# Value and gate panels as 512-column products, and another kind of unread product in the norms

## The chip, the cores and the metric

The kernel runs on one core of a Trainium2 chip. A core has TensorE (PE in the profile; its weight loads are listed as PEld), VectorE (DVE), ScalarE (ACT), GpSimd (POOL), and SyncE (SP), which here only issues DMAs. The metric is the device time of one execution in microseconds (us). The kernel before takes 2851.77 us, the median of 3 runs (2851.21 to 2854.91).

## The reference

256 tokens of width 1024 pass through two networks, one after the other. The first has two layers: multi-scale retention with a SwiGLU feed-forward, then a dilated attention with a second feed-forward, with a layer norm after each part. The second has two layers of a mixer (attention of 8 heads with forget gates, a 31-tap convolution, a gated linear recurrence) and a layer of 16384 small experts ("peer") of which each token uses 128, with rms norms ahead of them and one at the end. Cut to what the change touches:

```
retention:  q, k, v, gate = split(x @ w_in)        # gate and v: 4 heads x 512 columns
            y = norm(retain(rope(q), rope(k), v));  out = (silu(gate) * y) @ w_out
attention:  q, k, v of 3 groups x 16 heads x 64;    softmax over all keys of the 3 groups
mixer:      q, k, v = x @ w_in[:, :1536]            # 8 heads x 64 columns each
            out = concat(attend(q, k, v, f), conv, rnn) @ w_out
layer_norm: (x - mean) * rsqrt(var + eps) * g + b;  rms_norm: x * rsqrt(mean(x^2) + eps) * g
```

## The kernel before, in words

**Products.** Each float32 operand is split into two float32r parts, hi and lo (ScalarE rounds hi, VectorE subtracts to get lo), and a product is three float32r products: hi x hi, lo x hi, hi x lo. Weights come as panels [128, 1024] of 512 KB in the order of their use (class `Stream`): SyncE loads up to 4 ahead into `raw`, then `whi` and `wlo` have three buffers each. `W.ahead` emits the split of a later panel between the products of the present one.

Four shapes of product share the panels. `feat` gives features by tokens: the panel is stationary, 256 tokens move, 24 products per panel into one half of a bank. `nat` gives tokens by features for values and gates: the tokens are stationary, 256 columns of the panel move, two panels of 4 k-blocks make [2 halves of the tokens x 256 columns] in one bank, 24 products per panel, `mm(o, l[:, k, t], r[:, s], ...)`. `krow` and `krow_tail` are the sums over rows: 512 columns move, 12 products per panel, into four banks `acc`. There are 40 `nat` panels of x in retention (32) and the two mixers (4 each), and 24 in the attention.

**Banks.** `bank()` hands out two banks named `w` in turn for `feat`, `nat` and the unread products; a bank can be written again once its last reader (an ACTIVATE of 512 elements on ScalarE) is done. `sbank`, `spare` and `aux` are the other banks, for the small products.

**Order.** The program is emitted in the order of the main products. Small chains of work (a head's softmax, the convolution, the recurrence) are generators; `chains.run()`, called inside `feat` (3 times a panel), `nat` (4 times) and `krow` (2 times), emits a step of a chain when an estimate of time (`Clock`) says that its inputs are done. So where a step stands on each engine is decided by that estimate, and nothing is reordered later.

**Mixer.** `MIX_ORDER = "FCRAB"`: forget gate, convolution, recurrence, then A (queries and keys of heads pairs 0 and 1, then a `nat` for half of the values) and B (queries and keys of pairs 2 and 3, then a `nat` for the other half). The chains `heads(hp, ...)` of pairs 0 and 1 are added before A's `nat`, those of 2 and 3 before B's. Then come the `krow` products of the mixed features in the order `MIX_REST = (0, 1, 6, 7, 4, 5, 2, 3)` (0 to 3 heads, 4 and 5 convolution, 6 and 7 recurrence), the last three in `krow_tail`.

**Norms.** After each sum the tokens are normed on VectorE, ScalarE and GpSimd, transposed by TensorE, and copied from the banks by ScalarE into `xh` (four copies of [128, 4 blocks, 128 tokens]). While TensorE has nothing to do, `keep_warm(n)` gives it products that nobody reads, `mm(ps[:, :128], ident, ident, ...)` in float32: 14 in each layer norm (`WARM_LN`, the one that feeds mixer 0 among them), 8 in each other rms norm (`WARM_RMS`). In a layer norm they stand ahead of all transposes, in an rms norm between the transposes of the first 128 tokens and those of the others. The profile counts each of these as two instructions.

Of the kernel before, what the change touches and what calls it, by code (L numbers as in the profile page):

```python
# [13 lines left out]
AF = mybir.ActivationFunctionType  # L14
# [14 lines left out]
WARM_START = 18  # L29
LEAD = 2.4  # L30
# [3 lines left out]
EARLY = (0, 1)  # L34
# [15 lines left out]
class Stream:  # L50
    """Weight panels [128, 1024] in the order of their use: loaded ahead, split ahead into
    two float32r parts whose sum is the float32 panel."""
# [36 lines left out]
    def open(self, n):  # L89
        """The first panel, in n pieces."""  # L90
        self.step = 1024 // n
        for parts, name, dt, bufs in ((self.raw, "raw", F32, self.R), (self.hi, "whi", F32R, self.B),
                                      (self.lo, "wlo", F32R, self.B)):
            parts[0] = self.pool.tile([128, 1024], dt, name=name, bufs=bufs)
        self.nd = self.nh = self.nl = 1
# [13 lines left out]
    def ahead(self, part):  # L109
        """Further panels' parts, while the one that was got last is in use."""  # L110
# [5 lines left out]
    def take(self, k):  # L116
        """k panels to be used in any order, k at most the number of buffers."""
        self.lo_to(self.n + k)
        return [self._next() for _ in range(k)]
# [7 lines left out]
class Clock:  # L127
    """An estimate of when the instructions emitted so far are done, from their sizes, the order on
    their engines and the data they share."""
# [7 lines left out]
    def place(x):  # L137
        """The elements of a partition, as runs: their starts and their length."""
# [15 lines left out]
    def freed(self, slot, last):  # L154
        """When a bank's last tile has been read."""
# [57 lines left out]
class Timed:  # L213
    """An engine whose instructions the clock takes note of."""
# [23 lines left out]
class Chains:  # L238
    """Chains of work woven between the main products: a chain goes on when the clock says that its
    last step is done."""  # L240
# [4 lines left out]
    def add(self, gen, lane=None, rank=1, need=0):  # L245
        """Chains of a lane run one after the other; lower ranks go first. need: banks for the next step."""
# [42 lines left out]
def net(tc, A, out, stop=None):  # L289
# [3 lines left out]
    with ctx:  # L293
# [21 lines left out]
        def choice():  # L315
            """The chains' banks, by when they are free; while the sums' banks are unused, two of them also serve."""
# [54 lines left out]
        def feat(ps, xh, xl):  # L371
            """ps[feature, token] of one panel: weights stationary, tokens moving."""
# [8 lines left out]
        def nat(ps, xh, xl):  # L381
            """ps[token, c, 256 columns], K = 1024, two panels of 4 k-blocks."""
# [14 lines left out]
    
        def krow(acc, ah, al, first=False):
            """acc[c][half] += a^T panel for one k-block a [128, tokens] against 1024 columns."""
# [10 lines left out]
        def krow_tail(acc, parts, first=False):  # L410
            """The last three panels of such a sum, the first tokens before the others."""
# [17 lines left out]
        def rsqrt_wide(dst, v, a, b):  # L429
            """dst = 1 / sqrt(v): a first guess from the exponent, one step of second and one of third order."""  # L430
# [14 lines left out]
        class Turned:  # L445
            """xh, xl from the tokens' rows: the first part at once, the second in the end."""
# [18 lines left out]
        def to_T_flipped(c, h, dh, dl, src):  # L465
            """As to_T, the tokens from last to first."""
# [8 lines left out]
        def keep_warm(n):  # L475
            """Products nobody reads: the tensor engine's clock falls when it has nothing to do."""
            ps = bank()
            for _ in range(n):
                mm(ps[:, :128], ident, ident, start=True, stop=True)
# [3 lines left out]
        class Layer:  # L483
            """Layer norm of ALPHA times xN plus acc, in place."""
# [27 lines left out]
            def scale_beside(self, c, h):  # L512
                """As scale, on the other engines."""
# [40 lines left out]
        class Root:  # L554
            """xn[c] = rms norm of xN."""
# [24 lines left out]
        def rms(gb, xn, acc=None, then=None, first=None):  # L580
            """xn[c] = rms norm of xN, to which acc is added first; or of a layer norm."""
# [47 lines left out]
        # ------------------------------------------------------------------ retention  # L629
        def retention():  # L630
            with tc.tile_pool(name="ret", bufs=1) as p:
# [27 lines left out]
                def project(h):  # L659
# [7 lines left out]
                    for nm, f in (("v", AF.Copy), ("g", AF.Silu)):  # L667
                        r[nm] = p.tile([128, 2, 512], F32, name=nm + "_", bufs=2)
                        for j in range(2):
                            ps = bank()  # L670
                            nat(ps, xh, xl)
                            nc.scalar.activation(r[nm][:, :, j * 256:(j + 1) * 256],
                                                 ps.rearrange("p (c n) -> p c n", c=2), f)
# [66 lines left out]
        # ------------------------------------------------------------------ feed-forward  # L740
# [43 lines left out]
        # ------------------------------------------------------------------ dilated attention  # L784
        def bias_tiles(p):
            """scr[16 group + head, n]: the bias at distance n - 127, with the group's mask."""
# [18 lines left out]
        def attention(scr, xrh, xrl):  # L805
            """The three groups of a head share one softmax: weighting their outputs by the softmax of
            their log-denominators is the softmax over all their keys. Keys run from last to first."""
            with tc.tile_pool(name="att", bufs=1) as p:
# [18 lines left out]
                def heads(quad, hp, r):  # L827
                    """Two heads, side by side."""
# [54 lines left out]
                for quad in range(4):  # L883
                    r = {"n": 0, "b": bias_load(quad), "qk": p.tile([128, 3, 2, 2, T], F32, name="qk", bufs=2),
                         "v": p.tile([128, 3, 2, T], F32, name="v_", bufs=2)}
                    for kind, hp, g in att_order(quad):
                        ps = bank()
# [22 lines left out]
        # ------------------------------------------------------------------ second block: mixers  # L910
        def log1p_exp_neg(dst, az, th, s):
            """dst = log1p(exp(-az)) / 2, az >= 0: atanh((1 - t) / (3 + t)), t = tanh(az / 2)."""
# [11 lines left out]
        def decay_rates():  # L924
            """4 softplus(-lambda) and -8 softplus(-lambda) of both layers."""
# [742 lines left out]
```

## Time and profile before

| | us |
|---|---|
| median of 3 runs | 2851.77 |
| span of the profiled execution | 2850.2 |
| PE busy | 2802.1 (98%) |
| PEld busy | 2585.6 (91%) |
| DVE busy | 2015.7 (71%) |
| ACT busy | 1469.0 (52%) |
| POOL busy | 100.7 (4%) |

The profiled execution's own time is its span and what lies around the first and the last instruction; against the median of the runs that is 1.6 us more than the span. Retention fills about 8 to 213 us of the span, the first feed-forward to 411, the attention to 717, the second feed-forward to 916, mixer 0 929 to 1044, its experts to 1881, mixer 1 1888 to 2006, its experts to 2843. A matmul's duration in a row holds its way through the array, so consecutive ones overlap; what one costs in a row of many is the step from start to start.

### The profile page before, as it was taken

Reading aid. Unit: us, or ns where it says so; the run is one execution under the profiler, and the core shown is the slowest. Engines: PE = TensorE matmul, PEld = TensorE weight load, DVE = VectorE, ACT = ScalarE, POOL = GpSimd, SP = SyncE. Lnnn points to the kernel's source line nnn. Section 1 sums busy time; section 2 is a strip of 40 time slices with the busy share of each in tenths; the row PEclk is TensorE's granted clock in tenths of the full one; section 3 lists DMA queues with packets and bytes.
Section 4 is the critical chain, followed back from the end, with each engine's and each line's share of the span. In section 5 each row is a group of like instructions: output and inputs, shape, how many; then the busy total and the mean of one; then the engine's idle time right before and its main releaser. Section 6 shows DMA issues by size and latency. Waiting matters only on the chain.

```text
span 2850.2 us, 48921 instructions
## 1 busy us (share of the span) xinstructions
PE 2802.1 (98%) x19426; PEld 2585.6 (91%) x19426; DVE 2015.7 (71%) x3630; ACT 1469.0 (52%) x2343; POOL 100.7 (4%) x104
## 2 busy tenths in 40 slices
PE   9999999999999999999999999999999999999999
PEld 9988989998898889999998888888999999988887
DVE  5556566666656889988995555579898899755555
ACT  4444434554444654447764444455444577544444
POOL 1001010000101200000000000010000000000000
PEclk9999999999999999999999999999999999999999
DMA  7445556544554344554345555643455533455554
GB/s 242 163 163 179 186 167 205 173 145 139 191 187 161 120 150 161 193 182 137 127 140 182 195 193 192 202 161 117 157 184 186 170 127 130 160 191 193 192 194 161
DMA packets 135973, 484.25 MB, mean 170 GB/s; under 512 B 17152, under 2 KB 18176, under 8 KB 135744
## 3 DMA queue, kind: packets, MB, share of 16 engines
q1 hardware_dynamic: 132064, 468.07, 49.5%
q0 software_dynamic: 3680, 13.05, 1.5%
q8 instruction: 153, 2.51, 0.4%
q14 instruction: 76, 0.62, 0.1%
HBM read 479.92 MB, written 1.15 MB: 169 GB/s over the span
## 4 chain that ended last, share of the span: by engine, by line
PE 50%; issue 13%; DVE 2%; ACT 1%; POOL 0%; DVEq 0%; POOLq 0%; ACTq 0%
PE w L226 30%; PE acc L226 19%; DVE G L226 2%; PE b L226 1%; ACT G L226 0%; DVE wlo L226 0%; ACT whi L226 0%; DVE xN L226 0%; ACT ohb L226 0%; POOL r L226 0%; ACT xh L226 0%; POOL wlo L226 0%; POOL G L226 0%; ACT w L226 0%; DVE nm L226 0%
## 5 line engine op out<-in xcount | busy, mean ns | idle before, releaser
L226 DVE TENSOR_TENSOR wlo<-raw,whi 128x1024 fp32r<-128x1024 f32 (+1 forms) x874 | 1065.6, 1220 | 613.9 <-ACT whi L226 611.6
L226 ACT ACTIVATE whi<-raw 128x1024 fp32r<-128x1024 f32 (+1 forms) x881 | 926.7, 1053 | 750.8 <-PE acc L226 416.6
L226 PE MATMUL w<-xh,wlo 128*128 128x256 f32 x3568 | 506.3, 285 | 10.5 <-DVE wlo L226 10.4
L226 PE MATMUL w<-xl,whi 128*128 128x256 f32 x3568 | 509.7, 285 | 0.0
L226 PE MATMUL w<-xh,whi 128*128 128x256 f32 x3568 | 506.1, 284 | 1.4 <-ACT whi L226 1.0
L226 PEld LDWEIGHTS w<-xh,wlo 128*128 128x128 f32 x3568 | 460.3, 192 | 13.8 <-DVE wlo L226 12.7
L226 PEld LDWEIGHTS w<-xh,whi 128*128 128x128 f32 x3568 | 462.8, 192 | 5.1 <-ACT xh L226 1.6
L226 PEld LDWEIGHTS w<-xl,whi 128*128 128x128 f32 x3568 | 459.0, 191 | 2.4 <-issue 2.4
L226 PE MATMUL acc<-whi,xh 128*128 128x512 f32 x1024 | 317.3, 389 | 2.4 <-ACT xh L226 2.4
L226 PE MATMUL acc<-whi,xl 128*128 128x512 f32 x1024 | 317.3, 389 | 0.0
L226 PE MATMUL acc<-wlo,xh 128*128 128x512 f32 x1024 | 317.2, 389 | 0.0
L226 PEld LDWEIGHTS acc<-whi,xh 128*128 128x128 f32 x1024 | 192.1, 188 | 42.6 <-ACT xh L226 2.8
L226 PEld LDWEIGHTS acc<-whi,xl 128*128 128x128 f32 x1024 | 192.2, 188 | 40.0
L226 PEld LDWEIGHTS acc<-wlo,xh 128*128 128x128 f32 x1024 | 192.2, 188 | 39.8
L226 ACT ACTIVATE G<-w 128x512 f32<-128x512 f32 (+15 forms) x157 | 83.7, 533 | 203.2 <-PE w L226 202.8
L226 DVE TENSOR_SCALAR oha<-iota,e1T,gT 128x128 f32<-128x128 f32 x512 | 153.0, 341 | 0.0
L226 PE MATMUL acc<-ohb,oha 128*128 128x128 f32 x1024 | 136.6, 276 | 0.3
L226 PEld LDWEIGHTS acc<-ohb,oha 128*128 128x128 f32 x1024 | 125.9, 192 | 2.0 <-ACT ohb L226 1.4
L226 PE MATMUL w<-whi,xh 128*128 128x256 f32 x320 | 94.0, 294 | 0.0
L226 PE MATMUL w<-wlo,xh 128*128 128x256 f32 x320 | 92.5, 289 | 0.3
L226 PE MATMUL w<-whi,xl 128*128 128x256 f32 x320 | 92.2, 288 | 0.0
L226 POOL TENSOR_TENSOR r<-v,minus_half 128x1 f32<-128x1 f32 x26 | 21.9, 842 | 1965.6 <-DVE v L226 1965.6
(297 smaller groups left out, 3106.0 us busy)
## 6 DMA issues: line engine op xcount, KB each, us to landing
raw<-u SPq DMA_DIRECT2D x256, 512.0 KB, 3.5
raw<-v SPq DMA_DIRECT2D x256, 512.0 KB, 3.6
raw<-ffn SPq DMA_DIRECT2D x132, 512.0 KB, 3.7
raw<-mix SPq DMA_DIRECT2D x90, 512.0 KB, 3.5
raw<-att SPq DMA_DIRECT2D x80, 512.0 KB, 3.5
raw<-ret SPq DMA_DIRECT2D x63, 512.0 KB, 3.7
bias<-scr POOLq DMA_DIRECT2D x12, 512.0 KB, 8.0
G<-norm_g SPq DMA_DIRECT2D x4, 512.0 KB, 4.8
```

The costliest lines, as they stand in the source:

```text
L226: return f(*args, **kw)
```

## The change

Three edits. `wide` takes the place of `nat` in retention (all 32 panels), in the mixers (the two `nat` of a layer become one `wide` behind A's queries and keys) and in the attention for two of the three groups of a quad (16 of 24 panels): four panels of 2 k-blocks, 512 columns moving, one bank per half of the tokens, 12 products per panel. The values' and gates' panels are laid out for it (`wide_panels`). `keep_warm` multiplies parts of `xh` with each other in float32r, `2 * n` products of 128, 128, 192 and 192 columns in turn. In the mixers all heads' chains are added ahead of the values (`EARLY` is gone, it held both). The diff also drops docstrings and comments, which are left out here.

```
+WARM_N = (128, 128, 192, 192)
...
+        def wide(pss, xh, xl):
+            for p in range(4):
+                hi, lo = W.get()
+                for c in range(2):
+                    t = slice(c * 128, (c + 1) * 128)
+                    for i, (l, r) in enumerate(((xh, hi), (xh, lo), (xl, hi))):
+                        for j in range(2):
+                            k = 2 * p + j
+                            mm(pss[c], l[:, k, t], r[:, j * 512:(j + 1) * 512], start=(k == 0 and i == 0),
+                               stop=(k == 7 and i == 2))
+                    W.ahead(("hi", "lo")[c])
+                    chains.run()
...
         def keep_warm(n):
             ps = bank()
-            for _ in range(n):
-                mm(ps[:, :128], ident, ident, start=True, stop=True)
+            for i in range(2 * n):
+                mm(ps[:, :WARM_N[i % 4]], xh[:, 0, :128], xh[:, 1, :WARM_N[i % 4]], start=True, stop=True)
...
-                        for j in range(2):
-                            ps = bank()
-                            nat(ps, xh, xl)
-                            nc.scalar.activation(r[nm][:, :, j * 256:(j + 1) * 256],
-                                                 ps.rearrange("p (c n) -> p c n", c=2), f)
+                        pss = [bank(), bank()]
+                        wide(pss, xh, xl)
+                        for c, ps in enumerate(pss):
+                            nc.scalar.activation(r[nm][:, c], ps, f)
...
-                    ps = bank()
-                    nat(ps, xh, xl)
-                    nc.scalar.activation(v[:, :, j * 256:(j + 1) * 256], ps.rearrange("p (c n) -> p c n", c=2), AF.Copy)
-                    valued.add(j)
...
+                    if j == 0:
+                        pss = [bank(), bank()]
+                        wide(pss, xh, xl)
+                        for c, ps in enumerate(pss):
+                            nc.scalar.activation(v[:, c], ps, AF.Copy)
+                        valued.update((0, 1))
...
-    v = [("v", 0, g) for g in range(3)]
+    v = [("vv", 0, 0), ("v", 0, 2)]
     if quad in V_LAST:
         return qk[0] + qk[1] + v
-    return [x for pair in zip(qk[0], v) for x in pair] + qk[1]
+    return qk[0][:2] + v[:1] + qk[0][2:] + v[1:] + qk[1]
```

TensorE at the first values of retention, before; `xh` and `xl` are the tokens, `whi` and `wlo` the panel, `w` the bank:

```order
L226 MATMUL w<-xl,whi 128x256 x8
L226 MATMUL w<-whi,xh 128x256
L226 MATMUL w<-wlo,xh 128x256
L226 MATMUL w<-whi,xl 128x256
L226 MATMUL w<-whi,xh 128x256
L226 MATMUL w<-wlo,xh 128x256
L226 MATMUL w<-whi,xl 128x256
```

The same place in the changed kernel:

```order
L226 MATMUL w<-xl,whi 128x256 x8
L226 MATMUL w<-whi,xh 128x512 x2
L226 MATMUL w<-wlo,xh 128x512 x2
L226 MATMUL w<-whi,xl 128x512 x2
L226 MATMUL w<-whi,xh 128x512 x2
L226 MATMUL w<-wlo,xh 128x512 x2
L226 MATMUL w<-whi,xl 128x512 x2
```

Half as many products stand there, each twice as wide; the rest of retention's order on TensorE is as it was.

TensorE in the rms norm between mixer 0 and its experts, before, with what it waits for; `G` holds the normed tokens, `acc` and `b` are banks:

```order
L226 MATMUL acc_10562<-ident,G 128x128 [waits DVE_49]
L226 MATMUL acc_10562<-ident,G 128x128 x3
L226 MATMUL acc_10568<-ident,G 128x128 [waits DVE_49]
L226 MATMUL acc_10568<-ident,G 128x128 x3
L226 MATMUL w<-ident 128x128 [waits PE_49]
L226 MATMUL w<-ident 128x128 x7
L226 MATMUL b_10588<-ident,G 128x128 [waits DVE_49,PE_49]
```

And in the changed kernel:

```order
L226 MATMUL acc_9994<-ident,G 128x128 [waits DVE_49]
L226 MATMUL acc_9994<-ident,G 128x128 x3
L226 MATMUL acc_10000<-ident,G 128x128 [waits DVE_49]
L226 MATMUL acc_10000<-ident,G 128x128 x3
L226 MATMUL w<-xh 128x128 [waits Activation_49]
L226 MATMUL w<-xh 128x128
L226 MATMUL w<-xh 128x192 x2
L226 MATMUL w<-xh 128x128 x2
...
L226 MATMUL b_10028<-ident,G 128x128 [waits DVE_49,PE_49]
```

The unread products now read what ScalarE copies out of the first transposes, so they wait for ScalarE; the second transposes stand behind them as before. The rms norms ahead of mixer 1 and of its experts have the same wait; the layer norms and the last norm do not, since there no copy into `xh` stands ahead of the products.

TensorE around the end of B in mixer 0, before; `b` and `acc` with `G` are scores of heads pair 3 (64 and 8 rows), `mh` the mixed features:

```order
L226 MATMUL acc_10255<-G,ident 128x256
L226 MATMUL b_10256<-G,ident 128x256
L226 MATMUL w<-whi,xh 128x256
L226 MATMUL w<-wlo,xh 128x256
L226 MATMUL w<-whi,xl 128x256
L226 MATMUL w<-whi,xh 128x256
L226 MATMUL w<-wlo,xh 128x256
L226 MATMUL w<-whi,xl 128x256
L226 MATMUL b_10283<-G 128x256 x2
```

And in the changed kernel, the scores of pair 2 (the first eight rows with `b`) between two halves of the sum's first panel, those of pair 3 behind the second half:

```order
L226 MATMUL acc_9735<-whi,ml 128x512
L226 MATMUL b_9748<-G 128x128
L226 MATMUL b_9749<-G 128x128
L226 MATMUL b_9748<-G,ident 128x128
L226 MATMUL b_9749<-G,ident 128x128
L226 MATMUL b_9748<-G 128x256
L226 MATMUL b_9749<-G 128x256
L226 MATMUL b_9748<-G,ident 128x256
L226 MATMUL b_9749<-G,ident 128x256
L226 MATMUL acc_9736<-whi,mh 128x512
L226 MATMUL acc_9737<-whi,mh 128x512
```

Before, both pairs' scores, the convolution's statistics and pair 1's products with its values stood among the first 12 products of B's `nat`, with 36 of its products behind them; now the sum over the mixed features stands there. From pair 2's scores to its transposes TensorE now has 1 + 5 halves of a `krow` panel (36 products) and pair 3's scores.

## Rows read from the trace of the kernel before

**Rows 1.** The page: span, busy time and share of the engines.
```profile
span 2850.2 us, 48921 instructions
PE 2802.1 (98%) x19426; PEld 2585.6 (91%) x19426; DVE 2015.7 (71%) x3630; ACT 1469.0 (52%) x2343; POOL 100.7 (4%) x104
```

**Rows 2.** Groups by shape, products of `nat` (busy us, mean ns, idle before).
```profile
L226 PE MATMUL w<-whi,xh 128*128 128x256 f32 x320 | 94.0, 294 | 0.0
...
L226 PE MATMUL w<-whi,xrh 128*128 128x256 f32 x192 | 56.3, 293 | 0.0
```

**Rows 3.** Timeline (start, us), PE in retention's values, 108 products apart.
```profile
30.01 0.28 PE L226 MATMUL w<-wlo,xh 128*128 128x256 f32 x1
...
42.97 0.28 PE L226 MATMUL w<-wlo,xh 128*128 128x256 f32 x1
```

**Rows 4.** Windows (length, busy us and instructions), experts' sums; timeline, PE, a tail.
```profile
1600.00:1800.00 200.00, 200.00 (x884) 165.62 (x883) 112.56 (x111) 96.86 (x111) 0.00 (x0) 1.00 0.59 194
...
1036.13 0.40 PE L226 MATMUL acc<-whi,mh 128*128 128x512 f32 x1
...
1037.50 0.39 PE L226 MATMUL acc<-whi,mh 128*128 128x512 f32 x1
```

**Rows 5.** Timeline, ACT: a copy out of a bank in retention, one in the attention.
```profile
38.73 0.60 ACT L226 ACTIVATE g__439<-w 128x512 f32<-128x512 f32 x1 [0.52 <-PE w L226]
...
499.01 0.94 ACT L226 ACTIVATE s<-s,nm 128x768 f32<-128x768 f32 x1 [0.15 <-DVE nm L226]
...
499.94 0.58 ACT L226 ACTIVATE qk<-w 128x512 f32<-128x512 f32 x1
```

**Rows 6.** Timeline, PE in retention's layer norm.
```profile
212.90 3.29 PE L226 MATMUL w<-ident 128*128 128x128 f32 x28
216.02 0.60 PE L226 MATMUL acc<-ident,xN 128*128 128x128 f32 x4
217.33 0.66 PE L226 MATMUL acc<-ident,xN 128*128 128x128 f32 x4 [0.71 <-POOL xN L226]
221.38 1.75 PE L226 MATMUL b<-ident,xN 128*128 128x128 f32 x8 [3.39 <-DVE xN L226]
```

**Rows 7.** Timeline, the rms norm between mixer 0 and its experts.
```profile
1044.30 0.60 PE L226 MATMUL acc<-ident,G 128*128 128x128 f32 x4
...
1046.39 0.66 PE L226 MATMUL acc<-ident,G 128*128 128x128 f32 x4 [1.49 <-DVE G L226]
1046.88 1.95 PE L226 MATMUL w<-ident 128*128 128x128 f32 x16
...
1047.59 1.06 ACT L226 ACTIVATE xh<-acc 128x512 fp32r<-128x512 f32 x2
...
1049.49 1.23 PE L226 MATMUL b<-ident,G 128*128 128x128 f32 x8 [0.67 <-DVE G L226]
```

**Rows 8.** Windows: layer norm, rms norm, mixers 0 and 1 (after the busy times: granted clock).
```profile
222.00:225.40 3.40, 3.37 (x16) 3.27 (x16) 3.04 (x5) 2.84 (x4) 1.65 (x3) 0.51 0.71 254
...
1044.30:1051.00 6.70, 4.46 (x34) 3.64 (x33) 5.25 (x7) 3.13 (x8) 2.04 (x2) 1.00 0.26 81
...
1966.20:1969.60 3.40, 3.40 (x13) 1.92 (x12) 2.49 (x7) 0.90 (x2) 0.00 (x0) 0.51 0.22 89
1973.10:1976.50 3.40, 3.40 (x14) 3.04 (x13) 3.04 (x8) 2.17 (x11) 0.00 (x0) 0.50 0.00 0
...
974.30:1036.10 61.80, 60.78 (x390) 50.10 (x389) 57.25 (x112) 38.77 (x78) 0.00 (x0) 0.97 0.38 122
1932.80:1997.90 65.10, 64.08 (x391) 52.30 (x390) 57.61 (x112) 38.88 (x78) 0.00 (x0) 0.92 0.35 117
```

**Rows 9.** Timeline, PE in mixer 0: first scores of pair 2, and its transposes.
```profile
1004.90 0.37 PE L226 MATMUL b<-G 64*128 64x128 f32 x1
...
1022.35 0.82 PE L226 MATMUL b<-ident,G 128*128 128x128 f32 x6
```

**Rows 10.** Windows, mixer 0's middle (PE, PEld, DVE, ACT, POOL).
```profile
955.00:1030.00 75.00, 69.65 (x479) 60.24 (x477) 72.36 (x132) 45.60 (x89) 9.52 (x5) 0.98 0.36 120
```

More of the change, by code (lines that the diff above doesn't have):

```diff
@@ L33 @@
 N_LANES = 4
-EARLY = (0, 1)
 LEAD_BUILD = 0.8
@@ L886, in attention @@
                     for kind, hp, g in att_order(quad):
+                        if kind == "vv":
+                            pss = [bank(), bank()]
+                            wide(pss, xrh, xrl)
+                            for c, ps in enumerate(pss):
+                                nc.scalar.activation(r["v"][:, 0:2, c], ps.rearrange("p (g n) -> p g n", g=2), AF.Copy)
+                            r["n"] += 2
+                            continue
                         ps = bank()
@@ L1226, in mixers @@
                         nc.scalar.activation(t[:, 2 * j:2 * j + 2], pair(), AF.Copy, scale=sc)
-                    if j in EARLY:
-                        for i in range(2):
-                            chains.add(heads(2 * j + i, lanes[(2 * j + i) % N_LANES], j), (2 * j + i) % N_LANES, RANK_HEADS, 2)
-                    ps = bank()
-                    nat(ps, xh, xl)
-                    nc.scalar.activation(v[:, :, j * 256:(j + 1) * 256], ps.rearrange("p (c n) -> p c n", c=2), AF.Copy)
-                    valued.add(j)
-                    if j not in EARLY:
-                        for i in range(2):
-                            chains.add(heads(2 * j + i, lanes[(2 * j + i) % N_LANES], j), (2 * j + i) % N_LANES, RANK_HEADS, 2)
+                    for i in range(2):
+                        chains.add(heads(2 * j + i, lanes[(2 * j + i) % N_LANES], j), (2 * j + i) % N_LANES, RANK_HEADS, 2)
+                    if j == 0:
+                        pss = [bank(), bank()]
+                        wide(pss, xh, xl)
+                        for c, ps in enumerate(pss):
+                            nc.scalar.activation(v[:, c], ps, AF.Copy)
+                        valued.update((0, 1))
             while not {0, 1} <= done:
@@ L1584, in nat_panels, with wide_panels @@
     return w.reshape(2, 4, 128, -1, 256).transpose(3, 0, 2, 1, 4).reshape(-1, 128, 1024)
+def wide_panels(w):
+    return w.reshape(4, 2, 128, -1, 512).transpose(3, 0, 2, 1, 4).reshape(-1, 128, 1024)
 def row_panels(w):
@@ L1603, in lay @@
             [feat_panels(w[:, b + h * 256 + e:b + (h + 1) * 256:2]) for b in (0, 1024) for e in (0, 1)]
-            + [nat_panels(w[:, b + h * 512:b + (h + 1) * 512]) for b in (2048, 4096)]))
+            + [wide_panels(w[:, b + h * 512:b + (h + 1) * 512]) for b in (2048, 4096)]))
     a["ret"] = np.concatenate([per[0], per[1], per[2], o[0:4], per[3], o[4:16]])
@@ L1619, in lay @@
         for kind, hp, g in att_order(quad):
-            if kind == "v":
+            if kind == "vv":
+                seq.append(wide_panels(w[:, 2, 0:2, quad].reshape(1024, 512)))
+            elif kind == "v":
                 seq.append(nat_panels(w[:, 2, g, quad]))
@@ L1644, in lay @@
         for j, name in enumerate("AB"):
-            groups[name] = [cut(256 * j, 256, feat_panels), cut(512 + 256 * j, 256, feat_panels),
-                            cut(1024 + 256 * j, 256, nat_panels)]
+            groups[name] = [cut(256 * j, 256, feat_panels), cut(512 + 256 * j, 256, feat_panels)]
+        groups["A"].append(cut(1024, 512, wide_panels))
         a[f"mix{l}"] = np.concatenate([p for n in MIX_ORDER for p in groups[n]] + [o[i:i + 1] for i in MIX_REST]
```

## The prediction, made before the changed kernel ran

> **What bounds the kernel now.** I read the page first. PE is busy for 2802.1 of 2850.2 us, every other engine far less [rows 1], so an edit counts where it changes what TensorE does or waits for. Next the timeline of PE, from start to start, since a product's duration overlaps the next one's. In retention 108 products of 256 columns take 42.97 - 30.01 = 12.96 us, 0.120 us each, without an idle time between them [rows 3]: there a cheaper product is gained in full. Products of 512 columns step by 200/884 = 0.226 us in the experts' sums and by 1.37/6 = 0.228 us in a tail [rows 4]; I take 0.227. Third, the places where TensorE does wait: the norms [rows 6, 7], and the mixers, where VectorE is busy for 72.36 of 75 us [rows 10] and TensorE works among small products at a clock that is not always full [rows 8].
>
> **The wide products.** `nat` makes 3 x 320 + 3 x 192 = 1536 products [rows 2]. Those of the attention's third group stay, 4 quads x 48 = 192. The other 1344 become 672 of twice the width. A pair costs 2 x 0.120 = 0.240 us, the wide one 0.227: 0.013 us saved, 672 times, 8.7 us (8.1 with 0.228, 9.4 with 0.226). Of that 5.0 us fall in retention (384), 2.5 in the attention (192), 1.25 in the mixers (96). The columns are the same in number; what is saved is a part of each product that does not grow with them: 0.120 us less 256 columns at 2.4 GHz (0.107) leaves 13 ns, 0.227 less 512 (0.213) leaves 14.
>
> Here a rule speaks against the change. The Trainium skill (TensorE: Matmul & The Clock Gate, "Back-to-back issue gap") gives a warm product its columns over 2.4 GHz and about 2.5 ns more. By that rule the edit would save 672 x 2.5 ns = 1.7 us in place of 8.7. The trace of this kernel shows 13 to 14 ns at both widths, so I go by the trace.
>
> Splits, DMAs and ScalarE's copies stay as they are in number: a `wide` block is copied out in two instructions of 512 elements as two `nat` blocks were. The panels are used up every 12 x 0.227 = 2.7 us in place of 2.9, as the sums over rows already do.
>
> **The banks.** `wide` holds both banks. Its first 6 products (1.36 us) go into the bank that was filled a block earlier; the 7th needs the bank filled just before. In retention ScalarE waits for TensorE and copies at once, 0.60 us [rows 5]: hidden, 0.76 us to spare. In the attention the copy may stand behind exponentials of 0.94 us; behind two of them it ends after 2 x 0.94 + 0.58 = 2.5 us [rows 5], 1.1 us too late. Were that so at all four `vv`, 4.4 us; but ScalarE is half idle, and I take 0.3 for all.
>
> **The unread products in the rms norms.** In a layer norm they stand ahead of all transposes and wait for nothing new: 28 instructions took 216.02 - 212.90 = 3.12 us, 0.111 each, and behind them TensorE waits 0.71 and 3.39 us for GpSimd and VectorE [rows 6]. 28 products at 0.12 would take 3.4 us, hidden by these waits. In three of the four other rms norms the new wait costs: the first transposes start at 1046.39 at the latest and take under 0.5 us, the 16 old products ran from 1046.88, and the second transposes started at 1049.49, when VectorE was done [rows 7]. The new products read ScalarE's first copy into `xh`; two copies run from 1047.59 for 1.06 us [rows 7], so the first is done at about 1048.15. What is queued behind the waiting product is the second transposes, the copies of these, and the first panel of the next stage. No product of float32r below 256 columns stands in the trace. From below, 160 columns on average at 0.120/256 each give 0.075 us, 16 of them 1.2 us, end 1049.35: no cost. From above, at the price of the old float32 (two instructions of 0.111 for 128 columns, so 0.22, and 0.33 for 192; 0.28 on average) they take 4.5 us, end 1052.6, 3.1 us late, 9.4 us for three norms. The nearest rows are 0.111 (128 columns an instruction) and 0.120 (256, float32r); with 0.115 they end at 1050.0, 0.55 us late, three times: 1.7 us.
>
> The Trainium skill (same page, "LDWEIGHTS (loading the stationary operand)") prices a load by its 128 columns at 1.2 GHz, 107 ns, for any number of moving ones. By an estimate from that page 16 products take 1.7 us, and the three norms lose 1.2 us together. No row here shows such a product.
>
> **The clock in these norms.** Between 1044.30 and 1048.15 TensorE would now have 8 transposes alone, some 0.9 us of work in 3.9. Before it had them in 2.6 us and then the 16 products, and the granted clock stayed at 1.00 (2.4 GHz) [rows 8]. In the layer norm, after 4 transposes in 4 us, it fell to 0.5 (1.2 GHz) for 3.4 us [rows 6, 8]. The new stretch lies between. The price I read from the mixers: the same work takes 65.1 us in mixer 1 and 61.8 in mixer 0, and mixer 1 has two more such stretches, at 1966 and 1973 [rows 8]: 1.65 us each. Three norms, so 0 to 5.0 us; I take 0.8.
>
> **The mixers' order.** B's `nat` no longer stands behind the scores of pairs 2 and 3. Two things follow. The two stretches at half clock came where these scores and other small products stood close together; now products of 512 columns stand between the two pairs' scores. I count one of the two as gone, 1.7 us gained (0 to 3.3). Against it, pair 2's chain has less in front of it: from its scores to its transposes 17.4 us passed [rows 9], and now 36 products of 0.227, 8.2 us, and pair 3's scores stand there. At worst TensorE waits 17.4 - 8.2 = 9.2 us in each mixer. But those 17.4 us were mostly a queue: VectorE was busy all the while [rows 10] with the convolution, which the new order gives it ahead of the scores, and its work in sum is the same. I take 0.3 us a mixer, 0.6.
>
> **Sum.** -8.7 + 0.3 + 1.7 + 0.8 - 1.7 + 0.6 = -7.0 us. Against the profiled execution: a span of 2843.2, and with the 1.6 us around it 2844.8. The median of the runs shown is 2851.8, so this is 0.25% faster. What a measurement of this kernel can tell from no change is about 0.2%, 5.7 us: faster means below 2846.1, slower above 2857.5.
>
> **Rivals.** (B) Only the gains: the narrow products are cheap enough, the clock holds in the norms, both slow stretches of mixer 1 go: -8.7 - 3.3 + 0.5 = -11.5, 2840.3. For it: 0.67 us to spare behind the old products; against: the wait for ScalarE's copy is in the order.
>
> (C) The step of a wide product does not halve the fixed part, so that 2.5 ns are saved a pair: a gain of 1.7 us that the norms eat, 2851.8. That is what the page's rule gives; the steps of 0.120 and 0.226 to 0.228 speak against it.
>
> (D) The unread products cost as much as float32 ones: 9.4 us in the rms norms, and in the layer norms 28 x 0.28 = 7.8 us, which fills the wait until 221.38 and could save a slow stretch (1.65) in some of four: -8.7 + 9.4 + 0.6 - 3 = about -2, 2850. For it: nothing in the trace excludes it; against: 256 columns of float32r go at 0.120.
>
> (E) Slower: in both mixers TensorE runs out of sums before pair 2 and 3 are through their softmax. Place: from the first half of the first `krow` panel on. Price: up to 9.2 us a mixer, 2863; half of it gives 2854. It decides from (8.7 - 1.7)/2 = 3.5 us a mixer on, and beats the bound above from 6.4 on. For it: the cover that has gone; against: VectorE's total.
>
> **Chances.** The forecast 0.51, with its own range 2841.5 to 2848 (0.38 below 2846.1, 0.13 above); B 0.26, all faster; C 0.05 and D 0.11, both within 0.2%; E 0.07 (0.03 within, 0.04 slower). Faster 0.64, same 0.32, slower 0.04. The range reaches from 2838, B with the wide step at 0.226 and a little luck in the layer norms' clock, to 2852, past D: the unknown price of the narrow products makes its upper half.
>
> **What would show it.** In the profile after: steps of 0.227 from start to start in retention's values, and the stage shorter by 5.0 us at the end of its sums; only 192 products of 256 columns left in the attention's values. In the rms norms, the first unread product starting about 1.3 us after the first transposes end, and the second transposes late by 0.5 us. No stretch at half clock near the scores of pairs 2 and 3, and no idle time of TensorE above 1 us between its `krow` panels. A step of 0.240 for the wide ones, unread products of 0.2 us and more, or waits of several us for `mh` would make the prediction wrong.

## The result, and the profile after

The changed kernel takes 2865.9 us, median of 4 runs (2865.73 to 2871.09), beside 2851.72 (2851.21 to 2854.91) of the kernel before on the same chip, also 4 runs: 1.0052 times as long, 95% interval 1.0038 to 1.0066. It is slower by some 14 us, where 7 us less were forecast, and it lies outside the range.

The page of the kernel after, span and busy times, to set beside [rows 1]:

```profile
span 2864.2 us, 47567 instructions
PE 2804.0 (98%) x18754; PEld 2556.1 (89%) x18754; DVE 2017.6 (70%) x3630; ACT 1469.8 (51%) x2343; POOL 98.8 (3%) x104
```

672 instructions fewer on PE, as counted, and yet 1.9 us more of busy time and 14.0 us more of span. So PE waits 12 us longer; and since fewer instructions were not fewer busy microseconds, some of them ran slower.

The groups by shape of the kernel after, with [rows 2]: half as many products of twice the width; of the attention's 192 narrow ones 64 stay. The idle time now at the first of them names ScalarE.

```profile
L226 PE MATMUL w<-whi,xh 128*128 128x512 f32 x160 | 52.5, 410 | 1.2 <-ACT v__314 L226 0.8 <-ACT ropea L226 0.4
...
L226 PE MATMUL w<-whi,xrh 128*128 128x512 f32 x64 | 21.2, 412 | 0.0
```

The timeline of PE after, retention's last two wide blocks; the second line is the first sum over rows behind them. With [rows 3]:

```profile
150.90 0.63 PE L226 MATMUL w<-whi,xh 128*128 128x512 f32 x2
...
172.69 0.62 PE L226 MATMUL acc<-whi,yh 128*128 128x512 f32 x2
```

96 products in 21.79 us, 0.227 each, the step that was taken from the sums over rows. From the first product of the values to the start of the layer norm, retention is 2.5 us shorter (191.85 to 189.34). Later stages give it back: up to the first feature product behind it, the attention is 1.3 us longer, mixer 0 with its norm 7.2, the experts of layer 0 with the norm behind them 3.6, mixer 1 with its norm 3.6.

**The rms norm behind mixer 0**, timeline of PE and ACT after, with [rows 7]:

```profile
1048.78 0.60 PE L226 MATMUL acc<-ident,G 128*128 128x128 f32 x4
1050.86 0.66 PE L226 MATMUL acc<-ident,G 128*128 128x128 f32 x4 [1.48 <-DVE G L226]
...
1052.07 1.06 ACT L226 ACTIVATE xh<-acc 128x512 fp32r<-128x512 f32 x2
...
1052.70 3.47 PE L226 MATMUL w<-xh 128*128 128x128 f32 x16 [1.18 <-ACT xh L226]
1055.96 1.91 PE L226 MATMUL b<-ident,G 128*128 128x128 f32 x8
1057.71 0.58 PE L226 MATMUL w<-xh,whi 128*128 128x256 f32 x1
```

The unread products wait 1.18 us for the first copy into `xh`. They start 3.92 us behind the first transposes (3.85 forecast) and then take 3.26 us up to the next instruction, in place of the 1.84 that 16 times 0.115 would be. The windows after (length, PE busy, ..., granted clock, DMA share, GB/s), of this norm and of the one ahead of mixer 1, with [rows 8]:

```profile
1053.00:1059.80 6.80, 6.80 (x34) 6.56 (x33) 4.31 (x7) 2.62 (x5) 0.04 (x1) 0.50 0.02 5
1892.70:1899.50 6.80, 6.65 (x30) 6.42 (x31) 3.85 (x6) 2.36 (x5) 1.50 (x3) 0.50 0.06 22
```

The granted clock fell to 0.50 (1.2 GHz), where it had stayed at 1.00 before, and it stays there for the first 2 us of the next stage. The stretch before it held 8 transposes and 1.18 us more of idle time. The three norms take 8.93, 9.17 and 7.08 us in place of 6.51, 6.42 and 6.51. The third one, ahead of mixer 1's experts, waits as long, but the clock stays at 1.00 in it. Its timeline of PE and its window after:

```profile
2023.46 2.04 PE L226 MATMUL w<-xh 128*128 128x128 f32 x16 [1.18 <-ACT xh L226]
2025.33 1.04 PE L226 MATMUL b<-ident,G 128*128 128x128 f32 x8
...
2019.55:2026.62 7.07, 4.17 (x33) 3.45 (x31) 5.46 (x8) 2.93 (x8) 2.02 (x2) 1.00 0.22 81
```

There the products take 1.87 us and the norm 0.57 us more than before. So the wait by itself costs about 0.6 us a norm; what is more comes with the clock, and the same wait does not always bring it down.

**The last quad of the attention.** Timeline of ACT before: the copies of the quad's first two `nat`, each behind at most one pair of exponentials. TensorE waits for neither of them.

```profile
677.67 0.60 ACT L226 ACTIVATE v__6370<-w 128x512 f32<-128x512 f32 x1
...
683.43 0.60 ACT L226 ACTIVATE v__6370<-w 128x512 f32<-128x512 f32 x1 [1.75 <-PE w L226]
```

Timeline of PE and ACT after, with [rows 5]. The product at 682.68 is the first of the third group's `nat`, behind the quad's wide block:

```profile
679.28 0.61 PE L226 MATMUL w<-whi,xrl 128*128 128x512 f32 x2
681.12 0.94 ACT L226 ACTIVATE s<-s,nm 128x768 f32<-128x768 f32 x1 [0.15 <-DVE nm L226]
...
682.05 1.06 ACT L226 ACTIVATE v__5870<-w 128x512 f32<-128x512 f32 x2
682.68 0.39 PE L226 MATMUL w<-whi,xrh 128*128 128x256 f32 x1 [2.78 <-ACT v__5870 L226]
```

Both copies of the wide block stand behind a chain's exponentials, which waited for VectorE's `nm` themselves, and TensorE waits 2.78 us: the case for which the prediction had "1.1 us too late" as the worst.

**The mixers.** The same happens ahead of group B's queries. Timeline of PE and ACT after, mixer 0:

```profile
993.87 0.40 ACT L226 ACTIVATE G<-G,nm 128x128 f32<-128x128 f32 x1 [3.49 <-DVE nm L226]
994.89 0.49 PE L226 MATMUL acc<-ident,G 128*128 128x128 f32 x3
...
996.96 1.06 ACT L226 ACTIVATE G<-w 128x512 f32<-128x512 f32 x2
997.59 1.45 PE L226 MATMUL w<-xh,whi 128*128 128x256 f32 x8 [2.21 <-ACT G L226]
```

Right behind this wait, from 998.4 on, the clock is at 0.50 for 3.4 us. In the tail, among the last `krow` panels, TensorE waits for the softmax of pair 3 (0.15, 0.37, 0.91 and 0.21 us, 1.6 in all) where it waited 0.40 us before. The longest of these waits, first before and then after:

```profile
1033.10 0.73 PE L226 MATMUL acc<-whi,mh 128*128 128x512 f32 x2 [0.40 <-ACT mh L226]
```

```profile
1035.70 0.30 PE L226 MATMUL b<-ident,G 128*128 128x128 f32 x1 [0.91 <-DVE G L226]
```

And both mixers as a whole, windows from their first feature product to the first transposes behind their sums, first before and then after:

```profile
929.33:1044.30 114.97, 109.21 (x748) 95.79 (x749) 99.69 (x182) 67.99 (x124) 15.26 (x9) 0.99 0.41 138
1887.64:2006.01 118.37, 112.83 (x749) 98.03 (x750) 100.38 (x183) 66.99 (x123) 14.10 (x9) 0.96 0.40 134
```

```profile
929.00:1048.78 119.78, 111.23 (x701) 94.88 (x701) 100.00 (x182) 68.39 (x124) 15.16 (x9) 0.97 0.40 132
1898.12:2019.55 121.43, 114.37 (x702) 97.74 (x701) 100.12 (x182) 67.10 (x123) 12.92 (x9) 0.94 0.40 130
```

VectorE's work is the same (100 us), as the prediction held; TensorE's idle time is not (8.55 and 7.06 us, length less busy, against 5.76 and 5.54), nor is the clock.

### The profile page after: what moved, and what is told of

The parts are those of the page before. It is cut to its first block, busy times and chain, and to the rows that moved or that the text cites. A ratio compares the mean times of both kernels' runs of the same rounds, so it can differ in the third digit from the quotient of the medians.

```text
span 2864.2 us, 47567 instructions
## 1 busy us (share of the span) xinstructions
PE 2804.0 (98%) x18754; PEld 2556.1 (89%) x18754; DVE 2017.6 (70%) x3630; ACT 1469.8 (51%) x2343; POOL 98.8 (3%) x104
## 4 chain that ended last, share of the span: by engine, by line
PE 49%; issue 16%; DVE 2%; ACT 1%; POOL 0%; POOLq 0%; DVEq 0%; ACTq 0%
PE w L226 30%; PE acc L226 18%; DVE G L226 1%; PE b L226 1%; ACT G L226 0%; DVE xN L226 0%; ACT whi L226 0%; DVE wlo L226 0%; ACT ohb L226 0%; ACT xh L226 0%; POOL G L226 0%; POOL r L226 0%; ACT w L226 0%; DVE xl L226 0%; DVEq L1690 0%
## 5 line engine op out<-in xcount | busy, mean ns | idle before, releaser
L226 ACT ACTIVATE ohb<-iota,me2T 128x128 f32<-128x128 f32 x256 | 87.6, 392 | 0.7 <-PE acc L226 0.7
L226 DVE TENSOR_TENSOR xl<-G,xh 128x512 fp32r<-128x512 f32 x112 | 76.4, 684 | 0.0
L226 DVE TENSOR_TENSOR G<-G,acc 128x272 f32<-128x272 f32 (+22 forms) x128 | 66.6, 520 | 8.4 <-ACT H L226 8.2
```

What stands on the lines that cost most here:

```text
L226: return f(*args, **kw)
```

## Experiments

Each edit is told by itself, and each ratio is to the kernel before, run beside it on the same chip. Its interval is 0.0009 to 0.0014 to either side (2.6 to 4 us), so a difference of two kernels is known to 3.6 us at best.

**1. The unread products alone**, in the kernel before.

```
-  for _ in range(n):     mm(ps[:, :128], ident, ident, ...)
+  for i in range(2 * n): mm(ps[:, :WARM_N[i % 4]], xh[:, 0, :128], xh[:, 1, :WARM_N[i % 4]], ...)
```

> The kernel before with the new unread products as its only edit. Theory 1 (the norms cost what the trace of after shows between the sums' end and the next stage's first product: 8.93 in place of 6.51 us ahead of mixer 0's experts, 9.17 in place of 6.42 ahead of mixer 1, 7.07 in place of 6.50 ahead of mixer 1's experts, and about 1 us more in the products behind the first two, which still run at half clock): 5 to 8 us slower than before, 2857 to 2860. Rival (the unread products cost only their wait for ScalarE, 0.55 us a norm, and the half clock in the norms of after came from where the wide products moved the norms in time): 1 to 2.5 us slower, 2853 to 2854.5.

2858.28 us (2857.02 to 2860.36), 1.0020 (1.0011 to 1.0029): 5.7 us by the ratio. In the same norm, the timeline of PE of this run and then its window; the wait and the stretch at half clock are those of the full change. The three norms take 9.19, 9.18 and 8.14 us, 7.1 more than before in all; here the third one too is at half clock for 3.4 us.

```profile
1049.58 3.73 PE L227 MATMUL w<-xh 128*128 128x128 f32 x16 [1.18 <-ACT xh L227]
```

```profile
1049.60:1056.40 6.80, 6.80 (x31) 6.57 (x32) 4.00 (x6) 2.36 (x4) 0.32 (x1) 0.50 0.03 11
```

**2. The wide products alone**: the changed kernel with the old unread products.

```
-  for i in range(2 * n): mm(ps[:, :WARM_N[i % 4]], xh[:, 0, :128], xh[:, 1, :WARM_N[i % 4]], ...)
+  for _ in range(n):     mm(ps[:, :128], ident, ident, ...)
```

> The changed kernel with the old unread products (float32 products of the identity). Theory 1: the norms' part of the loss goes and the rest stays, 2865.9 - 7 = 2858 to 2860, still slower than before by 6 to 8 us, in the mixers (+4.3 and +2.6 us from the first value product to the sum's tail) and the attention (+1.3). Rival (the norms cost only their wait): 2863 to 2865.

2857.8 us (2854.24 to 2859.89), 1.0018 (1.0010 to 1.0027). This is a little less than the theory's 6 to 8 us. So the wide products, forecast at -8.7, cost 5 us as they are placed, and the unread ones the rest.

**3. The new unread products, reading `xl`**, which the norm writes only later, so that they wait for no copy.

```
-  mm(..., xh[:, 0, :128], xh[:, 1, :WARM_N[i % 4]], ...)
+  mm(..., xl[:, 0, :128], xl[:, 1, :WARM_N[i % 4]], ...)
```

> The changed kernel whose unread products read xl in place of xh: same shapes and type, but nothing that ScalarE has just written, so no wait for its copy in the rms norms. If the wait and the idle stretch before it are what costs (theory 1): as with the old products, 2858 to 2860, and the granted clock stays at 1.00 in the three rms norms. If the narrow float32r products themselves let the clock fall (rival): 2863 to 2866, with stretches at 0.5 in these norms.

2858.71 us (2857.76 to 2860.22), 1.0022 (1.0013 to 1.0031), as with the old products (1.0018). Timeline of PE of this run, and the window of the norm:

```profile
1052.16 2.01 PE L226 MATMUL w<-xl 128*128 128x128 f32 x16
1054.85 1.23 PE L226 MATMUL b<-ident,G 128*128 128x128 f32 x8 [0.68 <-DVE G L226]
```

```profile
1049.66:1056.17 6.51, 4.25 (x34) 3.46 (x32) 5.05 (x7) 2.95 (x8) 2.03 (x2) 1.00 0.27 91
```

The norm takes 6.51 us again, with 0.68 us to spare, and the clock stays at 1.00, in the two other norms too. So neither kind nor width of these products costs anything that can be measured; the wait for ScalarE's copy, and the fall of the clock that comes with it, does.

**4. The mixers as before**: wide products in retention and attention, old unread products, `nat` in the mixers behind A's and behind B's keys.

```
-  if j == 0: pss = [bank(), bank()]; wide(pss, xh, xl); ...
+  ps = bank(); nat(ps, xh, xl); ...                       # for A and for B, as before
```

> Wide products in retention and the attention alone; the mixers (two products of 256 columns wide blocks, order of chains) and the unread products as before. Theory 1 (the loss lies in the mixers' banks and order and in the norms): 2848 to 2851.5, that is retention 2 to 4 us shorter, the attention about 1 us longer through one wait of 2.8 us for a bank in the last quad. Rival (the wide blocks lose as much wherever they stand, through ScalarE's late copies): 2853 to 2856.

2852.16 us (2849.16 to 2856.6), 1.0000 (0.9991 to 1.0008): 5.1 us less than experiment 2, between the ranges of the theory and the rival. The mixers lose some 5 us. And what retention gains is eaten elsewhere: the attention up to its next stage takes 301.4 us (299.0 before), with a wait of 2.79 us in the last quad and a stretch at half clock behind it. (The wait stands in the changed kernel and in experiments 2, 3, 6 and 10 as well, the stretch behind it in 4 and 6 only.)

**5. The copies ahead of the chains**: experiment 2, and no chain goes on behind the last two panels of a wide block.

```
-  chains.run()
+  if p < 2: chains.run()
```

> The wide products with the old unread ones (2857.8 us), changed in one thing: behind the last two of a wide block's four panels no chain goes on, so that ScalarE's copies are ahead of the chains' next exponentials. Theory 1 (the wait for a bank behind a chain's exponentials costs): the waits of 0.74 us before B's queries in both mixers and of 2.79 us before the last quad's third value block are gone or shrink below 0.3 us, and the kernel takes 2852 to 2854 us. Rival (what the mixers lose comes from the late scores of pairs 2 and 3, seen in the waits of 0.9, 0.36 and 0.2 us among the last panels): these waits stay, and it takes 2856 us or more.

2871.11 us (2868.34 to 2872.87), 1.0058 (1.0044 to 1.0072), worse by 11 us than experiment 2: neither theory's number. The waits did go (0.09 us in the last quad, none ahead of B's queries). But the chains, started later, were missing further on. Timeline of PE of this run in mixer 0, and the window behind the wait:

```profile
1012.73 0.58 PE L226 MATMUL acc<-G 64*128 64x128 f32 x1 [3.09 <-ACT G L226]
```

```profile
1012.60:1033.10 20.50, 17.72 (x53) 11.18 (x54) 11.54 (x29) 6.81 (x21) 0.00 (x0) 0.50 0.02 7
```

20.5 us at half clock, the first 13.5 of them with small products alone. So in a mixer the wait at the bank does not decide alone; how the chains stand among the large products weighs more.

**6. The mixers' wide block behind B's keys** in place of A's; the rest as experiment 2.

```
-  if j == 0:                                             +  if j == 1:
-  groups["A"].append(cut(1024, 512, wide_panels))        +  groups["B"].append(cut(1024, 512, wide_panels))
```

> The wide products with the old unread ones (2857.8 us), but in both mixers the wide block stands behind the queries and keys of group B, as the values of B did before, in place of behind those of A. Theory (in the mixers the place counts: scores of pairs 2 and 3 without sums beside them, and a tail that waits for pair 3): the waits of 0.36, 0.9 and 0.2 us in the tails shrink to what they were before the change, under 0.3 us in all, so does the wait of 0.74 us before B's queries, and the kernel takes 2853 to 2855 us. Rival (the place does not count, only the two banks do): 2857 us or more; also if the products with the values of pairs 0 and 1, which come later now, make a tail wait instead.

2852.33 us (2850.24 to 2853.22), 0.9992 (0.9983 to 1.0001): 7 us less than experiment 2, with the same products, banks and copies. The expectation's reason was not quite right: the idle time of the mixers stays (7.04 us in each, 7.11 and 7.12 in experiment 2); what goes is time at half clock (table below).

**7. The last quad as before**: experiment 4 with three `nat` in the last quad.

```
 if quad in V_LAST:
-    return qk[0] + qk[1] + v
+    return qk[0] + qk[1] + [("v", 0, g) for g in range(3)]
```

> Wide products in retention and in the first three quads of the attention; the last quad's values, the mixers and the unread products as before the change (with the last quad wide too: 2852.2 us). Theory 1 (the last quad's third value block waits 2.79 us for a bank that ScalarE copies behind exponentials, and a stretch at half clock follows): attention is 3 to 4 us shorter, the kernel takes 2848 to 2849.5 us. Rival (the wait is that of the chain of exponentials itself, and comes back at another place): 2851 us or more.

2848.18 us (2846.52 to 2854.64), 0.9981 (0.9972 to 0.9990): 5.4 us less than experiment 4 for one block of values. The attention takes 298.0 us.

**8. Retention alone**: the kernel before with `wide` for retention's values and gates only.

```
-  for j in range(2): ps = bank(); nat(ps, xh, xl); ...   # v and g of retention
+  pss = [bank(), bank()]; wide(pss, xh, xl); ...
```

> The kernel before with wide products in retention alone: 384 products of 512 columns in place of 768 of 256. Theory 1 (a wide product steps by 0.227 us, two narrow ones by 0.240, less some 1.5 us of waits for banks and panels in head 0): retention is 3.5 to 4.5 us shorter and nothing behind it changes, 2847 to 2848.5 us. Rival (what the pitch saves is lost to the shared banks): 2851 us or more.

2850.41 us (2847.53 to 2852.02), 0.9987 (0.9978 to 0.9996): 3.7 us (1.1 to 6.3) of the 5.0 forecast. The blocks of heads 1 to 3 are each 1.1 to 1.25 us shorter (24.31 to 23.19 in head 2), 3.5 in all. Head 0's is 1.0 us longer (23.23 to 24.26), so that the trace shows 2.4 us: timeline of ACT and PE in this run,

```profile
32.57 1.06 ACT L227 ACTIVATE whi<-raw 128x1024 fp32r<-128x1024 f32 x1 [1.50 <-DMA raw<-ret]
33.53 1.07 ACT L227 ACTIVATE v__314<-w 128x512 f32<-128x512 f32 x2
34.16 0.73 PE L227 MATMUL w<-whi,xh 128*128 128x512 f32 x2 [0.78 <-ACT v__314 L227]
...
43.73 1.28 ACT L227 ACT_TABLE_LOAD   x1
45.02 1.09 ACT L227 ACTIVATE g__391<-w 128x512 f32<-128x512 f32 x2
```

ScalarE's queue holds the split of a panel that is still on its way from memory ahead of the copies, and later a table load. TensorE waits 0.60, 0.78 and 0.34 us for banks there. The table load takes 1.28 us, and the copy follows at once. The Trainium skill (ScalarE: Activation LUTs, "What ACT_TABLE_LOAD costs") states about 1283 ns, which the trace shows, and another 1380 ns for a drain, which no row here shows.

**9. Both places that paid**: experiment 6 with the last quad of experiment 7.

```
 # experiment 6, and
-    return qk[0] + qk[1] + v
+    return qk[0] + qk[1] + [("v", 0, g) for g in range(3)]
```

> The two places that paid, together: wide products in retention, in three quads of the attention (2848.2 us so far, 0.9981 of before) and in the mixers behind group B's keys (which gave 2852.3 with the last quad wide); old unread products. Theory (the place in the mixers decides, and the last quad's wait is gone): the parts add up, some 2 us less than with the mixers as before, 2845 to 2847 us, 0.997 to 0.998 of before. Rival (in the mixers nothing is gained, their time is set by the chains): 2848 to 2849 us.

2847.61 us (2845.25 to 2849.06), 0.9982 (0.9973 to 0.9991). It falls between the two expectations; as compared with experiment 7, nothing can be told to be gained in the mixers, except that the runs lie closer together.

**10. Narrow products, placed as the change places them**: experiment 4, with both `nat` of a mixer behind A's keys.

```
-  nat(ps, xh, xl)  # one half behind A, the other behind B
+  for i in range(2) if j == 0 else (): ps = bank(); nat(ps, xh, xl); ...
```

> Wide products in retention and attention, old unread products, and in the mixers narrow ones of 256 columns, but both halves of the values behind the keys of group A, where the change put them (with the mixers wide there 2857.8 us, with the mixers as before 2852.2 us). Theory P (the place costs: nothing but queries and keys beside the scores of pairs 2 and 3): 2856 to 2859 us, with the waits of 0.4 to 0.9 us in the tails. Theory W (the width costs: both banks of a wide block wait for ScalarE's copies): 2852 to 2853.5 us, and no wait before B's first query.

2862.18 us (2860.53 to 2866.85), 1.0033 (1.0021 to 1.0045): 9.4 us more than experiment 4. The width and the two banks are not what the mixers lose most by; the place is, and the loss is larger than expected. Windows of both mixers, and the timeline of PE in the first one's tail:

```profile
929.17:1050.93 121.76, 113.10 (x749) 98.45 (x749) 100.11 (x182) 68.02 (x124) 13.87 (x9) 0.95 0.38 129
1894.26:2020.89 126.63, 119.55 (x749) 102.21 (x750) 100.48 (x183) 66.89 (x123) 14.10 (x9) 0.91 0.37 125
```

```profile
1032.13 0.65 PE L227 MATMUL w<-G 128*64 128x256 f32 x2 [1.35 <-ACT G L227]
1034.73 1.54 PE L227 MATMUL w<-G 128*64 128x256 f32 x6 [1.96 <-DVE G L227]
```

**11. The last quad wide, the third group ahead of it**; the rest as experiment 9.

```
-    return qk[0] + qk[1] + [("v", 0, g) for g in range(3)]
+    return qk[0] + qk[1] + v[::-1]
```

> The kernel with both places that paid, but the last quad's values wide as well, the third group's narrow block ahead of the wide one, so that no block of the two banks follows the wide one: the sums over rows have banks of their own. Theory (the 2.79 us were the third block's wait for a wide block's banks): that wait is gone; at most the wide block's seventh product waits for the narrow one's copy, under 1.4 us; the time is within 1.5 us of that with the last quad as before, 2845 to 2848 us. Rival (ScalarE's exponentials delay the last chains in any case, whatever stands in front): 2850 us or more.

2847.31 us (2846.47 to 2848.17), 0.9980 (0.9971 to 0.9989), the least of all, though not to be told from experiment 9: 0.2% under the kernel before, 0.7% under the changed one. No wait above 0.3 us is left in the last quad; behind the wide block come sums that have banks of their own. Windows of both mixers in this run:

```profile
926.78:1042.95 116.17, 107.91 (x702) 92.75 (x702) 99.85 (x182) 68.18 (x124) 14.03 (x9) 0.99 0.41 136
1886.35:2002.15 115.80, 107.52 (x701) 92.30 (x702) 100.01 (x183) 66.90 (x123) 14.01 (x9) 1.00 0.41 137
```

**The mixers of all kernels together.** From one profile of each, the window of a mixer as above, its idle time (length less PE busy) and its time at half clock, as means over the mixers (experiment 5, which holds the chains back, is left out):

| values in the mixer | kernels | mixers | length, us | least to most | idle | at half clock |
|---|---|---|---|---|---|---|
| narrow, behind A and B | before, 1, 4, 7, 8 | 10 | 116.8 | 115.0 to 120.1 | 6.0 | 6.2 |
| wide, behind A | after, 2, 3 | 6 | 120.0 | 118.1 to 121.5 | 7.8 | 9.9 |
| narrow, behind A | 10 | 2 | 124.2 | 121.8 to 126.6 | 7.9 | 17.9 |
| wide, behind B | 6, 9, 11 | 6 | 116.0 | 115.8 to 116.5 | 7.5 | 3.1 |

I take a microsecond at half clock as half of one lost, since a stretch of 3.4 us cost 1.65 in [rows 8]. Wide behind A against narrow: 1.8 idle, 3.7 / 2 by the clock, less 0.6 for the pitch, the step from product to product (half of the 1.25 forecast for both mixers), 3.0 a mixer of 3.1 measured. Wide behind B: 1.4 idle, -3.1 / 2 by the clock, less 0.6: the -0.8 measured. The first line also shows that the same code runs 5 us apart from profile to profile, with the half-clock stretches; a single profile of a mixer proves little.

## Why the prediction was wrong

By differences of the ratios, times 2852 us, with the forecast behind each: retention -3.7 (-5.0); three quads of the attention -1.7 and the last quad +5.4 (together -2.2); the mixers +5.1 (-2.35); the unread products +9.7, 5.7 when alone (+2.5); together +14.8 (-7.0). Each is a difference of two kernels, so known to 3.6 us or so. Three terms failed: the mixers by 7.5 us, the attention's banks by 5.9, the unread products by 3.2 alone and 7.2 beside the wide ones.

**The wide products: right.** Steps of 0.227, 0.013 us saved a pair where nothing else waits. In retention's heads 1 to 3 this gave 3.5 us. By the rule of the Trainium skill that was weighed there (TensorE: Matmul & The Clock Gate, "Back-to-back issue gap") all four heads would have given an estimated 384 x 2.5 ns = 1.0 us; the trace does not agree. The Trainium skill gives this gap there for an isolated product and not for a stream of products with a weight load each, which is what stands here, so it was a weak rival.

**"ScalarE is half idle, and I take 0.3 for all": wrong.** A mean share was set against a queue served in order. Two places paid. One is the block behind the last quad's wide one, where a chain's exponentials, late by VectorE, stood ahead of both copies. The other is head 0 of retention, where it was a split waiting for its DMA. What the last quad cost is known only roughly: 5.4 us by experiment 7 beside 4, 2.9 and 3.4 by experiments 9 and 11 beside 6. In the traces, from its first feature product to its layer norm, the attention takes 287.8 us in experiment 7, 290.4 in the changed kernel with the wait, and 291.9 in experiments 4 and 6 with the wait and the stretch at half clock: 2.6 or 4.2 us. The upper bound of 4.4 us came near this by luck: it had four blocks of 1.1 us each, but one waited 2.78 us and the three others 0.13 at most. The block without slack is the last quad's: there the copies stand behind exponentials that wait for `nm` themselves. In experiment 11 no block of these two banks follows the wide one, and the wait is gone.

**"Three norms, so 0 to 5.0 us; I take 0.8": wrong in size.** The mechanism was named. The start of the products (3.92 against 3.85 us) and their price were right: the third norm, at full clock, lost 0.57 us, where the prediction had 0.55 (its own rows give 0.50). In the norm behind mixer 0 the clock made the rest of 2.42 us, and another 1 us in the next stage, whose first 2.1 us run at half clock. That is more than the 1.65 us of a stretch in the mixers, since this one is twice as long, 6.8 us. Three norms are 5.7 us longer in all. Why the unread products cost 9.7 us with the wide ones and 5.7 alone stays open. The norms do not show it: they are 5.7 us longer in the changed kernel's trace and 7.1 in experiment 1's. The changed kernel's mixers have more half clock than those of experiment 2, and waits of 2.2 us ahead of B's queries in place of 0.74; but experiment 3 has such waits too at the time of experiment 2, and a difference of 4.0 us is hardly more than the uncertainty.

**The mixers' "I count one of the two as gone, 1.7 us gained", and "0.6": wrong in sign.** Rival E, given 0.07, came nearest: the cover behind the scores of pairs 2 and 3 is gone, and 3 us a mixer are lost, near the 3.5 from which it was to decide. But its mechanism, a softmax that TensorE waits for, is the smaller part: 1.6 us in the tail in place of 0.4. Ahead of B's queries TensorE waits 0.7 to 2.8 us for a bank, and by the sum above 1.8 of the 3.0 us lost are the granted clock. The prediction took a stretch at half clock for something that wide products between the scores would cure; yet what had filled the time behind the last scores was B's `nat`, and with it gone the small products stand with fewer large ones beside them. Experiments 6 and 10 show that the place decides, and not the width or the two banks: the same wide block behind B has the least half clock of all, and narrow ones behind A have the most. Why the place acts on the clock is read from the order of the products alone; no run changed the clock by itself.

The forecast failed in one more way: all three costs were known by name with bounds of 4.4, 5.0 and 18.4 us, and for each a value near the lower end was taken. The forecast needed all three to be low at once.

## What to carry to other kernels

A product that costs less is worth its saving only where the next user of its banks, and the small work that leaned on it as cover, do not change with it: look at the instruction behind the block on the copying engine's queue, not at that engine's busy share. Products that keep the clock up should depend on nothing that is late itself; here those of stale data did it at no measurable cost. And when a block is moved in a stage woven with small products, try its place apart from its form: in the two mixers here the place was worth 7 us with wide products and 9 with narrow ones, the form 1.25 by its step.

## What the runs showed of the hardware

Behind a wait of 1.18 us between transposes the granted clock fell to 1.2 GHz for 6.8 us, in a norm that had held 2.4 GHz with unread products in that place; in the third rms norm of the same trace the same wait left it at 2.4 GHz. Float32r products of 128 and 192 columns cost about what as many instructions of float32 with 128 did: 16 take 2.01 us (experiment 3), against 1.95 [rows 7]. And the same instructions of a mixer take 115.0 to 120.1 us from one profile to the next, with 1.1 to 11.2 us of half clock in them.
